# Sums of weight blocks: from accumulating DRAM transfers to VectorE additions, in a two-layer encoder on one core

## The chip, the cores and the metric

The kernel runs on one core of a Trainium2 chip. The metric is the device time of one execution in microseconds; the median of three executions is given. Engines by the names of the profile: PE (TensorE, matrix products), PEld (its weight loads), DVE (VectorE), ACT (ScalarE), POOL (GpSimd), SP (SyncE, which issues most transfers). Sixteen DMA engines move data between DRAM (HBM) and the on-chip memory SBUF; transfers that SP issues are on queue q1, those that GpSimd issues on queue q0.

## The reference

A two-layer encoder in float32 over 16 + 256 = 272 tokens of width 2048. One layer, cut to what matters here:

```python
h = rmsnorm(x)
q, k, v, f, ga, gf = split(h @ w_in)
a_br = attention(q, k, v) @ w_attn_br
s_br = real(fft2(f)) @ w_four
x = x + (sigmoid(ga) * a_br + sigmoid(gf) * s_br) @ w_out
h2 = rmsnorm(x)
up = h2 @ w_up                       # (272, 2 * 5632)
u_gate = dwconv3(up[:, :5632])
u_val = up[:, 5632:]
x = x + (silu(u_gate) * u_val) @ w_down
```

The output is the 256 real tokens after the second layer, whose feed-forward therefore needs 256 tokens only.

## The kernel before

**Weights as chunks.** All weights are read once, in the order in which TensorE uses them, as chunks of 128x1024 float32, 512 KB each. `order` (L172) lists the groups of matmuls with their chunks. For each chunk, SP loads it into a buffer `raw` (L233 to L245, four buffers), ScalarE rounds it to `wh` (L280), VectorE computes the rest `wl` = raw - wh (L283, three buffers each), and TensorE multiplies three times, with `wh` and the activations' high part, `wh` and their low part, `wl` and their high part (L352 to L354): 24 matmuls to a chunk. `advance` and `pump` keep the splits two chunks ahead of TensorE (LOOK = 2) and the loads four buffers ahead of these. In layer 0 the Fourier weights are folded by two VectorE additions before their split (`fold_w`, L268).

**Stages.** In the time of the profile: layer 0's projections, attention and Fourier part, gates and output projection up to about 540 us; its feed-forward (264 chunks: `ps_ug`, `ps_uv`, `ps_d`) to about 1336 us; layer 1's mixing part to about 1830 us; its feed-forward to the end.

**Block products.** The second feed-forward computes part of its products, those of `w_dn` (most rows of `w_down`) and `w_vn` (part of `w_up`), by a seven-product scheme on 2x2 blocks of weights, in place of eight products (`PRODUCTS`, L52). Four of the seven need sums of weight blocks. With w(h, k) for block k of column half h:

- sum 0 = w(0,0) + w(1,0)
- sum 1 = sum 0 + w(1,1)
- sum 2 = w(1,1) + w(1,0)
- sum 3 = w(0,1) + sum 1

They are made in DRAM, `fv` (4 x 8 chunks) for `w_vn`, `ft` (4 x 20 chunks) for `w_dn`, and layer 1 loads them as ordinary chunks (112 of them).

**How the sums are made.** `weight_sums` (L533) is a generator. For each sum and pair of chunks it lets GpSimd issue a transfer from DRAM to DRAM that copies the first summand (1 MB), and then another that adds the second summand to it in DRAM (`accum_op`). Ahead of each issue stands a one-column copy `tick` on GpSimd that reads the last `wl` (L538), so that the transfer starts in step with the splits. 56 copies and 56 accumulations.

**Pace.** `step` (L294) is called after every six matmuls of a chunk of 24 (four steps to a chunk). It advances one background generator of the list `shadow` whose count has run out, and, separately, `weight_sums`, every `slow[2]` steps: 15 to 45, set by stage, from the first Fourier gate of layer 0 until the sums are done in layer 1's feed-forward.

**Folds.** `prefold` (L513) runs in the background of the first feed-forward. It loads 32 chunks of layer 1's Fourier weights (`pfi`) over SP's queue, folds each by four VectorE additions of 128x256 (L528) and stores it to `fw` over SP's queue, one in about 28 steps.

**Order.** Instructions of an engine run in the order of its queue. A scheduler places most of them; those under `keep_in_program_order` stay in the order of the program among themselves.

Of the kernel before, what the change touches and what calls it, by code (L numbers as in the profile page):

```python
# [10 lines left out]
F32 = mybir.dt.float32  # L11
F32R = mybir.dt.float32r
AF = mybir.ActivationFunctionType
ALU = mybir.AluOpType
AX = mybir.AxisListType

P = 128
# [5 lines left out]
KT = D // P  # L23
# [3 lines left out]
NG = 8  # L27
# [5 lines left out]
CW = 4  # L33
MG = 2
FF_SPLIT = (24, 20)
SETS = (12, 8)
NQ = sum(SETS)
# [19 lines left out]
NV = KT // 2  # L57
# [3 lines left out]
FIRSTS = [sum(SETS[:i]) for i in range(len(SETS))]  # L61
# [6 lines left out]
def _branch(text):  # L68
# [3 lines left out]
BRANCH_ORDER = (  # L72
    _branch("ga0 ga1 ga2 ga3 gf0 gf1 s0 gf2 a0 s1 gf3 a1 s2 ga4 a2 s3 gf4 a3"),
    _branch("s4 a4 ga5 gf5 s5 a5 ga6 gf6 s6 a6 ga7 gf7 s7 a7"),
)
# [83 lines left out]
def encoder_kernel(ctx, tc, xT, params, consts, bmat, cfold, csign, w_fl, w_f64c, w_in, w_abr, w_four, w_f64, w_out, w_up, w_down, w_vn, w_dn, w_dt, out):  # L159
    nc = tc.nc  # L160
# [5 lines left out]
    fw = dram.tile([2 * KT, P, CW, MG * P], F32, name="fw")  # L166
    ft = dram.tile([4, NQ, P, CW, MG * P], F32, name="ft")
    fv = dram.tile([4, NV, P, CW, MG * P], F32, name="fv")
# [4 lines left out]
    for l in range(DEPTH):  # L173
# [13 lines left out]
        for half in range(2):  # L187
            for kind, j in BRANCH_ORDER[half]:
                w, off, n = {"ga": (w_in, IN_GA, KT), "gf": (w_in, IN_GF, KT), "s": (w_four, 0, 8), "a": (w_abr, 0, 8)}[kind]
# [24 lines left out]
    chunks, folded, mix, summed = [], set(), {}, {}  # L214
    t, done = 0, 0
    for key, chs in order:
        for j, ch in enumerate(chs):
            n = 0
            if key[0] == 1 and key[1] in ("t", "ug", "uv"):
                n = due(t) - done  # L220
                t += 1
            if n:
                mix[key, j] = n
                for s, p, k in PRODUCTS[done:done + n]:
                    if p in (3, 4, 5, 6):
                        summed[len(chunks)] = (s > 0, (3, 0, 1, 2)[p - 3], k // 2)
                    chunks.append(pchunks[done])
                    done += 1
                first_mix = min(first_mix, len(chunks) - n) if done > n else len(chunks) - n
            if key[:2] == (0, "s"):  # L230
                folded.add(len(chunks))
            chunks.append(ch)
    st = {"raw": 0, "fetch": 0, "next": 0, "grp": 0}  # L233
# [13 lines left out]
    todo, ready_sums = [], set()  # L247
# [26 lines left out]
    def split_w(i, a, b, parts="hl"):  # L274
        if i not in splits:
            splits[i] = tuple(wp.tile([P, CW, MG * P], F32R, tag=t, name=f"{t}{i}") for t in ("wh", "wl"))
        h, lo = splits[i]
        r = raws[i]
        if "h" in parts:
            nc.scalar.copy(h[:, a:b], r[:, a:b])  # L280
        st["wl"] = lo
        if "l" in parts:
            nc.vector.tensor_tensor(lo[:, a:b], r[:, a:b], h[:, a:b].bitcast(F32), op=ALU.subtract)  # L283
            if b == CW:
                del raws[i]
# [3 lines left out]
    def push(gen, wait=0):  # L289
        shadow.append([wait, gen])  # L290

    slow = [0, None, 0]

    def step(force=False):  # L294
        if not force and slow[1] and slow[2]:
            slow[0] -= 1
            if slow[0] <= 0:
                slow[0] = slow[2]
                if next(slow[1], None) is None:
                    slow[1] = None  # L300
        for s in shadow:
            s[0] -= 1
        for s in list(shadow):
            if force or s[0] <= 0:
                try:
                    s[0] = next(s[1])
                except StopIteration:
                    shadow.remove(s)
                return
# [5 lines left out]
    def drain():  # L315
        while shadow:
            step(True)
# [136 lines left out]
    small = ctx.enter_context(tc.tile_pool(name="small", bufs=4))  # L454
# [55 lines left out]
        norm_split(m, goff)  # L510
        norm_sum(m)

    def prefold(pool):  # L513
        src = [w_fl[k] for k in range(KT)] + [w_four[1, j, c] for j in range(NG) for c in range(2)]
        outs = {}
        for j in range(len(src) + 1):
            if j < len(src):
                a = pool.tile([P, CW, MG * P], F32, tag="pfi", name=f"pfi{j}", bufs=2)
                nc.sync.dma_start(a, src[j])
            if j:  # L520
                nc.sync.dma_start(fw[j - 1], outs.pop(j - 1))
            yield 15
            if j < len(src):
                o = pool.tile([P, CW, MG * P], F32, tag="pfo", name=f"pfo{j}", bufs=2)
                for q, op in ((0, ALU.add), (1, ALU.subtract)):
                    for c in range(2):
                        half = (lambda t_, e: t_[:, 2 * c:2 * c + 2, e * P:(e + 1) * P]) if j < KT else (lambda t_, e: t_[:, 2 * e + c])
                        tc.keep_in_program_order(nc.vector.tensor_tensor(half(o, q), half(a, 0), half(a, 1), op=op))  # L528
                        yield 3
                outs[j] = o  # L530
            yield 1

    def weight_sums():  # L533
        rows = lambda ap: ap.rearrange("k p c m -> (k p) (c m)")

        def issue(out_, s, **kw):
            tick = small.tile([P, 1], F32, tag="tick", name="tick", bufs=1)
            tc.keep_in_program_order(nc.gpsimd.tensor_copy(tick, st["wl"][:, 0, 0:1].bitcast(F32)))  # L538
            tc.keep_in_program_order(nc.gpsimd.dma_start(out_, s, **kw))

        for f, wd, nq, q0, n in [(fv, w_vn, NV, 0, NV)] + [(ft, w_dn, NQ, q0, n) for q0, n in zip(FIRSTS, SETS)]:
            dst = lambda q, j: rows(f[q, 2 * j:2 * j + 2])
            w = lambda h, k, j: rows(wd[h, nq * k + 2 * j:nq * k + 2 * j + 2])
            kinds = ((0, lambda j: w(0, 0, j), lambda j: w(1, 0, j)),
                     (1, lambda j: dst(0, j), lambda j: w(1, 1, j)),
                     (2, lambda j: w(1, 1, j), lambda j: w(1, 0, j)),
                     (3, lambda j: w(0, 1, j), lambda j: dst(1, j)))
            for q, base, more in kinds:
                j0, j1 = q0 // 2, (q0 + n) // 2
                for j in range(j0, j1 + 1):  # L550
                    if j < j1:
                        issue(dst(q, j), base(j))
                        yield 1
                    if j > j0:
                        issue(dst(q, j - 1), more(j - 1), accum_op=ALU.add, max_dma_last_dim=4096)
                        ready_sums.add((f is ft, q, j - 1))
                        yield 1

    def norm_stats(holder, gap=0):
        am = small.tile([P, P // NM, NM], F32, tag="am", name="am", bufs=1)  # L560
# [23 lines left out]
        holder["tok2"] = tok2  # L584

    xr = lambda lo: (lambda kt: (xH[:, kt, lo:T], xL[:, kt, lo:T]))
    slow[1] = weight_sums()

    for l in range(DEPTH):
        last = l == DEPTH - 1  # L590
        lo = 14 if last else 0
# [4 lines left out]
        with tc.tile_pool(name=f"mix{l}", bufs=1) as mp:  # L596
# [567 lines left out]

            tha, thf, w64s = {}, {}, []
            for half in range(2):
                slow[2] = 0
                mH = mL = None
                for n_, (kind, i) in enumerate(BRANCH_ORDER[half]):
                    if half or n_ >= (8 if last else 4):  # L1170
                        slow[2] = 26 if last else 15
                    j = i - 4 * half
                    if kind == "ga":
                        tha[i] = gate("ga", i)
# [16 lines left out]
                    else:  # L1191
# [7 lines left out]
                        for m in range(MG):  # L1199
                            k = 2 * j + m  # L1200
                            t_, h_ = tha[i][:, m, lo:T], mH[:, k, lo:T]
# [1 line left out]
                            nc.vector.tensor_tensor(t_, t_, thf[i][:, m, lo:T], op=ALU.add)  # L1203
                            nc.scalar.copy(h_, t_)
                            nc.vector.tensor_tensor(mL[:, k, lo:T], t_, h_.bitcast(F32), op=ALU.subtract)  # L1205
                slow[2] = 22 if last else 20 if half else 15
                for mg in range(8):
                    ps = group((l, "o", half, mg), lambda kt: (mH[:, kt, lo:T], mL[:, kt, lo:T]), W)
                    for m in range(MG):
# [6 lines left out]
        with tc.tile_pool(name=f"ffn{l}", bufs=1) as fp:  # L1216
            hold = {}
            push(norm_stats(hold), 8)
            if not last:
                push(prefold(fp), 8)  # L1220
            def conv_gate(i):
                ps = group((l, "ug", i), xr(lo), W)
                until(hold, "tok2")
# [23 lines left out]
            for c, n in enumerate(() if last else FF_SPLIT):  # L1247
                gHL = fp.tile([P, FF_SPLIT[0], 2, T], F32R, tag="gHL", name="gHL")
                gH, gL = gHL[:, :, 0, :], gHL[:, :, 1, :]
                for i in range(k0 // MG, (k0 + n) // MG):  # L1250
                    cs = conv_gate(i)
                    ps = group((l, "uv", i), xr(0), T)
                    for m in range(MG):
                        j = 2 * i + m - k0
# [7 lines left out]
                        if c == len(FF_SPLIT) - 1:  # L1262
                            norm_in(mt, P_NM + (l + 1) * KT)
                k0 += n
            if not last:
                slow[2] = 0

            if last:
                X0, X1 = 26, 32
                XF = XT.rearrange("p k t -> p (k t)")  # L1270
# [16 lines left out]
                left = {(h, b): (1 if h == 1 and b < 2 else 2) * len(SETS) + 1 for h in range(2) for b in range(4)}  # L1287
# [84 lines left out]
                def products():  # L1372
                    late = []
                    until(hold, "tokens")
                    slow[2] = 45
                    make_ahead()
                    bank.extend([psum.tile([P, 512], F32, tag="aux", name=f"ps_p{i}{h}") for h in range(2)] for i in range(2))
                    for s_, p, q in PRODUCTS:
                        ps = bank[(p in (4, 2, 1)) ^ s_ % 2]
                        fresh = p in (0, 4, 1)  # L1380
                        wh, wl = (w.rearrange("p c m -> p (c m)") for w in next_split())
                        direct = s_ == 0 and p in plain
                        if direct:
                            k, h = plain[p]
                            a, b = xH[:, k + q, xt[h]], xL[:, k + q, xt[h]]
                        else:
                            a, b = made.pop((s_, p, q))
# [12 lines left out]
                        if (s_, q) in END:  # L1400
                            while late:
                                hand_out(*late.pop(0))
                            t_, c, minus = {0: (0, 0, 0), 4: (1, 2, 0), 5: (0, 2, 1), 2: (0, 2, 0), 6: (1, 2, 1), 1: (0, 0, 0), 3: (1, 0, 0)}[p]
# [4 lines left out]
                        yield  # L1408
                    assert not late

                slow[2] = 18
                st["products"] = products()
                st["pool"] = fp
                for i in UP_ORDER:
# [14 lines left out]
                    for m in range(0 if i in VPAIRS else MG):  # L1429
                        j = 2 * i + m  # L1430
                        cv = cs[m][:, lo2:T]
                        v = fp.tile([P, W2], F32, tag="v", name="v", bufs=2)
# [16 lines left out]
                for b in TAIL_ORDER:  # L1449
                    k, chs = order[st["grp"]]  # L1450
# [95 lines left out]
```

## Time and profile before

| | us |
|---|---|
| median of 3 runs | 2542.17 (2540.26 to 2542.8) |
| span of the profiled execution | 2544.3 |
| PE busy in it | 2528.2 (99%) |
| DVE busy | 1825.0 (72%) |
| ACT busy | 1319.8 (52%) |
| POOL busy | 132.3 (5%) |

The profiled execution's own time is its span; around it lies nothing that the profile shows, and the runs without a profile are about 2 us shorter. Matmuls overlap in the pipeline, so the busy time of PE is the time in which at least one was under way, and it says nothing of how fast each one ran; the windows give the number of matmuls beside it. DMA share is the mean over 16 engines of the time that packets took; packets on one engine can overlap, so that a short window can show more than 1.

A row of windows reads: stretch, its length, then busy time and (xcount) of PE, PEld, DVE, ACT and POOL, then granted TensorE clock, DMA share, and GB/s moved. A row of waits reads: who waited, at which tile and line, for whom: total us, times, longest us. A row of DMA queues reads: packets, MB, share. A row of issues reads: destination and source, queue, count, KB each, median us from issue to landing.

### The profile page before, as it was taken

The numbers are of one execution on the slowest core, as the hardware profiler recorded it, in microseconds if no ns is written. First come the engines' busy times: TensorE is split into PE (matmuls) and PEld (weight loads), VectorE is DVE, ScalarE is ACT, GpSimd is POOL, SyncE is SP. The second block draws the span as 40 slices with busy tenths as digits, with TensorE's granted clock in tenths as the row PEclk, the third lists the DMA queues.
The fourth block names the chain that finished last, engine by engine and source line by source line (L and its number), as shares of the span: only waits on it lengthen the run. The fifth ranks groups of instructions, "written<-read, shape, count | busy, mean of one in ns | idle before, by whom it ended". The sixth has DMA issues, their size and how long they took to land.

```text
span 2544.3 us, 47646 instructions
## 1 busy us (share of the span) xinstructions
PE 2528.2 (99%) x18992; PEld 2447.4 (96%) x18992; DVE 1825.0 (72%) x2889; ACT 1319.8 (52%) x1893; POOL 132.3 (5%) x265
## 2 busy tenths in 40 slices
PE   9999999999999999999999999999999999999999
PEld 8999999999999999999999999999988999888987
DVE  7687766776666556666558877666778778777788
ACT  5455434554444334444445555444676566656565
POOL 0000100000000000000000000000000000000000
PEclk9999999999999999999999999999999999999999
DMA  6546889989989998999875646887889888887787
GB/s 238 163 156 217 261 270 288 280 262 302 308 271 305 300 306 274 281 318 294 252 247 183 201 150 209 246 266 240 260 293 282 298 274 285 288 286 264 240 268 261
DMA packets 171215, 660.69 MB, mean 260 GB/s; under 512 B 19424, under 2 KB 24672, under 8 KB 170096
## 3 DMA queue, kind: packets, MB, share of 16 engines
q1 hardware_dynamic: 152528, 538.07, 61.3%
q0 software_dynamic: 17024, 117.45, 18.7%
q8 instruction: 149, 2.44, 0.4%
q10 hardware_dynamic: 1440, 2.13, 0.2%
q14 instruction: 74, 0.61, 0.1%
HBM read 635.91 MB, written 136.31 MB: 304 GB/s over the span
## 4 chain that ended last, share of the span: by engine, by line
PE 86%; DMA 2%; DVE 1%; ACT 1%; issue 0%; ACTq 0%; DVEq 0%
PE ps_p L1390 10%; PE ps_ug L353 7%; PE ps_ug L354 7%; PE ps_ug L352 7%; PE ps_uv L348 4%; PE ps_d L353 3%; PE ps_uv L353 3%; PE ps_d L352 3%; PE ps_uv L354 3%; PE ps_d L354 3%; PE ps_uv L352 3%; PE ps_o L353 2%; PE ps_o L354 2%; PE ps_o L352 2%; PE ps_uv L349 2%; PE ps_gf L354 2%
## 5 line engine op out<-in xcount | busy, mean ns | idle before, releaser
L283 DVE TENSOR_TENSOR wl<-raw,wh 128x1024 fp32r<-128x1024 f32 (+1 forms) x937 | 1129.7, 1217 | 567.5 <-ACT wh L280 559.5
L280 ACT CAST wh<-raw 128x1024 fp32r<-128x1024 f32 (+1 forms) x937 | 976.0, 1046 | 890.8 <-PE ps_ug L353 201.2
L353 PE MATMUL ps_ug<-xHL,wh 128*128 128x272 f32 (+1 forms) x1408 | 401.9, 285 | 0.0
L354 PE MATMUL ps_ug<-xHL,wl 128*128 128x272 f32 (+1 forms) x1408 | 401.4, 285 | 0.4 <-DVE wl L283 0.4
L352 PE MATMUL ps_ug<-xHL,wh 128*128 128x272 f32 (+1 forms) x1408 | 400.8, 285 | 0.0
L353 PEld LDWEIGHTS ps_ug<-xHL,wh 128*128 128x128 f32 x1408 | 264.7, 188 | 3.2
L352 PEld LDWEIGHTS ps_ug<-xHL,wh 128*128 128x128 f32 x1408 | 264.6, 188 | 3.2
L354 PEld LDWEIGHTS ps_ug<-xHL,wl 128*128 128x128 f32 x1408 | 264.7, 188 | 0.6 <-DVE wl L283 0.6
L353 PE MATMUL ps_uv<-xHL,wh 128*128 128x272 f32 x704 | 203.3, 289 | 0.0
L353 PE MATMUL ps_d<-gHL,wh 128*128 128x272 f32 x704 | 202.9, 288 | 0.0
L352 PE MATMUL ps_d<-gHL,wh 128*128 128x272 f32 x704 | 202.9, 288 | 0.0
L354 PE MATMUL ps_uv<-xHL,wl 128*128 128x272 f32 x704 | 202.6, 288 | 0.0
L352 PE MATMUL ps_uv<-xHL,wh 128*128 128x272 f32 x704 | 202.3, 287 | 0.0
L354 PE MATMUL ps_d<-gHL,wl 128*128 128x272 f32 x704 | 202.1, 287 | 0.0
L1390 PE MATMUL ps_p<-wh,opnd 128*128 128x512 f32 x688 | 187.8, 394 | 0.0
L348 PE MATMUL ps_uv<-xHL,wh 128*128 128x512 f32 x448 | 159.8, 395 | 0.0
L353 PE MATMUL ps_o<-mL,wh 128*128 128x272 f32 (+1 forms) x512 | 146.6, 286 | 1.3 <-DVE mL L1205 1.3
L352 PE MATMUL ps_ga<-xHL,wh 128*128 128x272 f32 (+1 forms) x512 | 147.8, 289 | 0.0
L352 PE MATMUL ps_gf<-xHL,wh 128*128 128x272 f32 (+1 forms) x512 | 146.9, 287 | 0.1
L354 PE MATMUL ps_gf<-xHL,wl 128*128 128x272 f32 (+1 forms) x512 | 146.0, 285 | 0.4 <-DVE wl L283 0.4
L353 PE MATMUL ps_ga<-xHL,wh 128*128 128x272 f32 (+1 forms) x512 | 146.1, 285 | 0.0
L353 PE MATMUL ps_gf<-xHL,wh 128*128 128x272 f32 (+1 forms) x512 | 146.1, 285 | 0.0
(372 smaller groups left out, 5871.4 us busy)
## 6 DMA issues: line engine op xcount, KB each, us to landing
raw<-in_w_up SPq DMA_DIRECT2D x320, 512.0 KB, 5.2
raw<-in_w_in SPq DMA_DIRECT2D x191, 512.0 KB, 4.2
raw<-in_w_down SPq DMA_DIRECT2D x88, 512.0 KB, 5.4
raw<-ft SPq DMA_DIRECT2D x80, 512.0 KB, 4.8
raw<-in_w_out SPq DMA_DIRECT2D x64, 512.0 KB, 5.6
ft<-in_w_dn POOLq DMA_DIRECT2D x30, 1024.0 KB, 12.0
raw<-in_w_dn SPq DMA_DIRECT2D x60, 512.0 KB, 4.7
raw<-in_w_abr SPq DMA_DIRECT2D x32, 512.0 KB, 4.8
```

What stands on the lines that cost most here:

```text
L280: nc.scalar.copy(h[:, a:b], r[:, a:b])
L283: nc.vector.tensor_tensor(lo[:, a:b], r[:, a:b], h[:, a:b].bitcast(F32), op=ALU.subtract)
L348: nc.tensor.matmul(o2, h[:, c, sl], ab, start=kt == 0, stop=False)
L349: nc.tensor.matmul(o, lo[:, c, sl], ab[:, 0, :], start=False, stop=kt == nk - 1)
L352: nc.tensor.matmul(o, h[:, c, sl], a, start=kt == 0, stop=False)
L353: nc.tensor.matmul(o, h[:, c, sl], b, start=False, stop=False)
L354: nc.tensor.matmul(o, lo[:, c, sl], a, start=False, stop=kt == nk - 1)
L1390: nc.tensor.matmul(ps[h], x, w[:, 512 * h:512 * h + 512], start=fresh and (s_, q) in BEGIN and first, stop=(s_, q) in END and end, skip_gr ...
```

## The change

`weight_sums`, `prefold`, the tick copies, `slow` and its settings go. In their place stands one generator `prepare`, which is pushed to the background list at the start of the first feed-forward. It first does the 32 folds, then the 112 sums, one chunk of 512 KB at a time. GpSimd issues all its transfers, loads and stores between DRAM and seven SBUF buffers `ws`. A fold is the same four additions as before. A sum is made in place on VectorE, in two additions of 128x512, from chunks that are in SBUF: each of the four blocks of a position is loaded once, and sums 1 and 3 take the sum made before them from its buffer. A fold's load is issued two jobs ahead, a sum's load four jobs ahead, and a job takes seven steps, every fourth one six. So all folds and sums now lie in the first feed-forward, and none elsewhere.

```diff
-        st["wl"] = lo
...
-    slow = [0, None, 0]
-
     def step(force=False):
-        if not force and slow[1] and slow[2]:
-            slow[0] -= 1
-            if slow[0] <= 0:
-                slow[0] = slow[2]
-                if next(slow[1], None) is None:
-                    slow[1] = None
...
-    def prefold(pool):
...
-    def weight_sums():
...
+    def prepare(pool):
+        tt = lambda *v, **kw: tc.keep_in_program_order(nc.vector.tensor_tensor(*v, **kw))
+        dma = lambda *v: tc.keep_in_program_order(nc.gpsimd.dma_start(*v))
+        tile_ = lambda n: pool.tile([P, CW, MG * P], F32, tag="ws", name=n, bufs=7)
+        folds = [(w_fl[k], k) for k in range(KT)] + [(w_four[1, j, c], KT + 2 * j + c) for j in range(NG) for c in range(2)]
+        sums = []
+        for f, wd, nq in ((fv, w_vn, NV), (ft, w_dn, NQ)):
+            for k in range(nq):
+                sums += [(wd[h, nq * e + k], (f, q, k)) for h, e, q in ((0, 0, 0), (1, 0, 2), (1, 1, 1), (0, 1, 3))]
+
+        def fold(held, n, j):
+            a, o = held[n], tile_(f"wo{n}")
+            for q, op in ((0, ALU.add), (1, ALU.subtract)):
+                for c in range(2):
...
+                    tt(half(o, q), half(a, 0), half(a, 1), op=op)
+                    yield 1
+            dma(fw[j], o)
+
+        def sum_up(held, n, f, q, k):
+            x, y = held[n], held[n + (1, -2, 1, -1)[q]]
+            for c in (0, 2):
+                tt(x[:, c:c + 2], x[:, c:c + 2], y[:, c:c + 2], op=ALU.add)
+                yield 1
+            dma(f[q, k], x)
+            ready_sums.add((f is ft, q, k))
+
+        for jobs, ahead, work in ((folds, 2, lambda h, n, to: fold(h, n, to)), (sums, 4, lambda h, n, to: sum_up(h, n, *to))):
+            held = {}
+            for n in range(len(jobs) + ahead):
+                if n < len(jobs):
+                    held[n] = tile_(f"wi{n}")
+                    dma(held[n], jobs[n][0])
+                left = 7 - n % 4 // 3
+                if n >= ahead:
+                    for v in work(held, n - ahead, jobs[n - ahead][1]):
+                        left -= v
+                        yield v
+                yield left
...
-    slow[1] = weight_sums()
...
-                push(prefold(fp), 8)
+                push(prepare(fp), 8)
```

More of the change, by code (lines that the diff above doesn't have):

```diff
@@ L225, in encoder_kernel @@
                     if p in (3, 4, 5, 6):
-                        summed[len(chunks)] = (s > 0, (3, 0, 1, 2)[p - 3], k // 2)
+                        summed[len(chunks)] = (s > 0, (3, 0, 1, 2)[p - 3], k)
                     chunks.append(pchunks[done])
@@ L511, in norm_in @@
         norm_sum(m)
-    def prefold(pool):
[L514 to L531, printed above, removed]
@@ L533, in weight_sums @@
-    def weight_sums():
[L534 to L557, printed above, removed]
@@ new lines, in prepare @@
+    def prepare(pool):
[11 more added lines that the diff above has]
+                for c in range(2):
+                    half = (lambda t_, e: t_[:, 2 * c:2 * c + 2, e * P:(e + 1) * P]) if j < KT else (lambda t_, e: t_[:, 2 * e + c])
+                    tt(half(o, q), half(a, 0), half(a, 1), op=op)
[20 more added lines that the diff above has]
+                yield left
@@ L1166, in encoder_kernel @@
             for half in range(2):
-                slow[2] = 0
                 mH = mL = None
-                for n_, (kind, i) in enumerate(BRANCH_ORDER[half]):
-                    if half or n_ >= (8 if last else 4):
-                        slow[2] = 26 if last else 15
+                for kind, i in BRANCH_ORDER[half]:
                     j = i - 4 * half
@@ L1205, in encoder_kernel @@
                             nc.vector.tensor_tensor(mL[:, k, lo:T], t_, h_.bitcast(F32), op=ALU.subtract)
-                slow[2] = 22 if last else 20 if half else 15
                 for mg in range(8):
@@ L1264, in encoder_kernel @@
                 k0 += n
-            if not last:
-                slow[2] = 0
             if last:
@@ L1374, in products @@
                     until(hold, "tokens")
-                    slow[2] = 45
                     make_ahead()
@@ L1409, in products @@
                     assert not late
-                slow[2] = 18
                 st["products"] = products()
```

## The prediction

> **What bounds the kernel now.** I read the page first, then the waits of TensorE, then the stages by windows, then the DMA queues of single stages. The page:
>
> ```profile
> span 2544.3 us, 47646 instructions
> PE 2528.2 (99%) x18992; PEld 2447.4 (96%) x18992; DVE 1825.0 (72%) x2889; ACT 1319.8 (52%) x1893; POOL 132.3 (5%) x265
> ...
> q1 hardware_dynamic: 152528, 538.07, 61.3%
> q0 software_dynamic: 17024, 117.45, 18.7%
> ```
>
> TensorE is idle for 2544.3 - 2528.2 = 16.1 us. No edit changes its list of matmuls, so 16.1 us, plus what the clock lost, is all there is to win, while any starving is a loss. Queue q0 holds only the weight sums. Its 117.45 MB take 18.7% of the engines' span, so 18.7 / 117.45 = 0.159% per MB; q1 pays 61.3 / 538.07 = 0.114%. The waits of TensorE, whole span:
>
> ```profile
> PE ps_f L420 <- ACT wh L280: 4.7, 2, 4.4
> PE ps_a L354 <- DVE wl L283: 2.8, 2, 2.6
> PE ps_s L388 <- DVE wl L283: 1.4, 2, 0.8
> PE ps_o L353 <- DVE mL L1205: 1.3, 1, 1.3
> PE ps_fa L652 <- DVE E L631: 1.1, 1, 1.1
> PE ps_ug L354 <- DVE wl L283: 0.4, 1, 0.4
> PE ps_gf L354 <- DVE wl L283: 0.4, 1, 0.4
> PE ps_uv L349 <- DVE wl L283: 0.3, 1, 0.3
> ```
>
> `ps_f` (start of the program), `ps_o` and `ps_fa` wait for something other than a weight split; the change touches none of them. The five waits for `wl` come to 2.8 + 1.4 + 0.4 + 0.4 + 0.3 = 5.3 us. Where they sit, in windows of 10 us in the mixing part of layer 0:
>
> ```profile
> 240.00:250.00 10.00, 10.00 (x82) 10.00 (x81) 6.19 (x12) 3.50 (x5) 0.69 (x2) 1.00 1.01 360
> 260.00:270.00 10.00, 9.96 (x81) 9.82 (x80) 8.00 (x17) 5.14 (x10) 0.69 (x2) 1.00 1.10 351
> 270.00:280.00 10.00, 7.41 (x52) 7.19 (x52) 4.48 (x7) 2.76 (x4) 0.00 (x0) 0.90 0.49 159
> 280.00:290.00 10.00, 10.00 (x78) 10.00 (x78) 9.11 (x17) 6.04 (x12) 1.45 (x2) 0.93 0.85 225
> 300.00:310.00 10.00, 9.00 (x70) 8.57 (x69) 7.90 (x13) 4.30 (x6) 0.70 (x2) 1.00 0.99 369
> ```
>
> The columns are the length, PE, PEld, DVE, ACT and POOL busy, granted clock, DMA share, GB/s. DMA is full (1.01 to 1.10) just before TensorE falls to 7.41 of 10 us, and after that gap the clock is 0.90 and 0.93, another 10 x (0.10 + 0.07) = 1.7 us. In the stretch from 203 to 330 us the waits and the queues say why:
>
> ```profile
> DVE wpm L271 <- DMA raw<-in_w_four: 13.8, 3, 6.2
> ```
>
> ```profile
> q0 software_dynamic: 1385, 10.92, 31.5%
> ...
> raw<-in_w_four SPq DMA_DIRECT2D x8, 512.0 KB, 7.2
> ```
>
> VectorE waits up to 6.2 us for Fourier weights that land 7.2 us after issue, while the weight sums hold 31.5% of the DMA engines. Everywhere else TensorE is full. The first feed-forward, about 540 to 1336 us, is where all sums will go (same columns; the last row is the end of the kernel with almost no q0):
>
> ```profile
> 540.00:829.00 289.00, 289.00 (x2307) 288.92 (x2307) 192.46 (x301) 132.31 (x172) 18.59 (x39) 1.00 0.90 295
> 829.00:1000.00 171.00, 171.00 (x1365) 171.00 (x1364) 91.98 (x121) 63.01 (x65) 10.89 (x24) 1.00 0.92 296
> 1000.00:1215.00 215.00, 215.00 (x1719) 215.00 (x1718) 143.18 (x220) 95.62 (x123) 13.09 (x28) 1.00 0.91 294
> 1215.00:1336.00 121.00, 121.00 (x966) 121.00 (x965) 67.61 (x90) 53.74 (x72) 7.28 (x18) 1.00 0.80 248
> ...
> 2220.00:2500.00 280.00, 280.00 (x1660) 248.03 (x1658) 221.19 (x277) 173.99 (x218) 0.71 (x1) 1.00 0.81 266
> ```
>
> TensorE has not one idle microsecond there; a matmul takes 289 / 2307 = 0.125 us, a chunk of 24 matmuls 3.01 us, a background step (six matmuls) 0.75 us. DMA is at 0.90, so this is also the stage with least room.
>
> **Removed outside the first feed-forward.** All 56 copies, 56 accumulations and 112 tick copies on GpSimd go, from 203 us to 2220 us. GpSimd is at 5%, so ticks cost nothing now. What the path wins is the waits for `wl`, 5.3 us, and the clock's 1.7 us: 7.0 us. Bounds: 0, if the Fourier chunks are late by their own burst, and 16.1 + 1.7 - 4.7 - 1.3 - 1.1 = 10.7 us, if everything but the three foreign waits went. I take 6: the stalls stand right behind full DMA windows, and without a third of the load the chunks should land as they do in quieter stretches, but each still needs two fold additions on VectorE.
>
> **Moved and added: transfers.** In the first feed-forward the weights are 264 chunks of 512 KB (0.524 MB), 138 MB; the folds 32 loads and 32 stores, 34 MB, now on GpSimd's queue instead of SP's; the sums 112 loads and 112 stores, 117 MB. Together 289 MB in 796 us, 364 GB/s, against (289x295 + 171x296 + 215x294 + 121x248) / 1000 = 229 MB now. The price of a MB is what matters:
>
> ```profile
> q1 hardware_dynamic: 17851, 65.00, 62.8%
> q0 software_dynamic: 2771, 19.92, 27.2%
> ...
> raw<-in_w_up SPq DMA_DIRECT2D x91, 512.0 KB, 6.2
> pfi<-in_w_fl SPq DMA_DIRECT2D x15, 512.0 KB, 6.7
> ft<-in_w_dn POOLq DMA_DIRECT2D x7, 1024.0 KB, 12.1
> fw<-pfo SPq DMA_DIRECT2D x13, 512.0 KB, 5.4
> ```
>
> These are 540 to 829 us. Plain traffic: 0.628 x 289 us for 65.0 MB, 358 GB/s at share 1. Sums as they are now: 0.272 x 289 for 19.92 MB, 253 GB/s. A store (5.4 us to landing) is no dearer than a load (6.7). At the plain price 289 MB need 807 us of 796, a share of 1.01. That alone does not stop TensorE, because the share adds up packets that overlap, and goes above 1:
>
> ```profile
> 720.00:728.00 8.00, 8.00 (x66) 8.00 (x65) 7.09 (x12) 4.26 (x7) 0.76 (x2) 1.00 1.18 455
> 932.00:956.00 24.00, 24.00 (x193) 24.00 (x192) 12.20 (x15) 8.42 (x8) 1.78 (x4) 1.00 1.03 363
> 1392.00:1416.00 24.00, 23.95 (x207) 23.38 (x206) 23.32 (x33) 16.90 (x26) 0.12 (x1) 1.00 0.83 258
> ```
>
> From 932 to 956 us 363 GB/s pass, the rate needed on average, at full TensorE, with dear accumulations among them; 455 GB/s pass for 8 us. From below the cost is 0. From above, the last stage's 266 / 0.81 = 328 GB/s as a ceiling gives 289 / 0.328 = 881 us, 85 us more. I take 0: the 24 us row is nearest in rate and mix.
>
> The Trainium skill (DMA: Bandwidth & Descriptors, Specifications) gives a core about 358 GB/s of HBM bandwidth; by it the stage would take 289 / 0.358 = 807 us, 11 us longer. The rows of 363 and 455 GB/s speak against that as a hard limit over 24 and 8 us; no run here shows 364 GB/s over 796 us.
>
> **Added: VectorE.** 112 sums in two halves are 224 additions of 128x512. The nearest rows (the first fence for the whole program, the second for 545 to 1336 us):
>
> ```profile
> L280 ACT CAST wh<-raw 128x1024 fp32r<-128x1024 f32 (+1 forms) x937 | 976.0, 1046 | 890.8 <-PE ps_ug L353 201.2
> ...
> L271 DVE TENSOR_TENSOR wpm<-raw 128x512 f32<-128x512 f32 x32 | 21.1, 688 | 20.9 <-DMA raw<-in_w_four 20.7
> ```
>
> ```profile
> L283 DVE TENSOR_TENSOR wl<-raw,wh 128x1024 fp32r<-128x1024 f32 x263 | 322.2, 1225 | 276.2 <-ACT wh L280 274.9 <-issue 0.7
> L528 DVE TENSOR_TENSOR pfo<-pfi 128x256 f32<-128x256 f32 x128 | 51.6, 419 | 0.0
> ```
>
> 224 x 0.688 = 154 us onto 495 us of VectorE (the four windows), 649 of 796, 82%. Tightest is the start, where the 32 folds, spread over 680 us now, come one in 6.75 steps, 5.1 us: 4 x 0.419 = 1.68 us in 5.1 (33%) where before it was about 8%, so 192 / 289 = 67% becomes some 92%. From 1392 to 1416 us VectorE ran at 97% and TensorE lost 0.05 us. The splits run two chunks ahead of TensorE, 6 us, less a cast of about 1.05 us and a split of 1.2 us: nearly 4 us of backlog before a matmul waits. I take 0 for it, 10 us as the bad end (6% of the 170 us that the folds last).
>
> **Added: waits.** On VectorE an addition now waits for its load, and behind it in order stands the next `wl` split, for which TensorE waits. A sum's second operand is asked for three jobs ahead, 15 us, a fold's operand at least 14 steps, 10.5 us, against 6.7 us landing for such a load now. On GpSimd a load waits for the store that frees its buffer, at the closest two jobs earlier, 10 us against 5.4; behind it stand only transfers of this kind. GpSimd issues 288 transfers; a present issue is
>
> ```profile
> L539 POOL DMA_DIRECT2D ft<-in_w_dn x60: 502/728/955, 589.3 to 2156.1; - x60
> ```
>
> 288 x 0.73 = 210 us of 760: covered. SP is rid of 64 transfers and keeps the order of the rest. The last sum stands beside chunk 425 of the chunks 168 to 431, about 20 us before the stage ends, so nothing of layer 1 waits.
>
> **The sum.** 2544.3 - 6 = 2538 for the profiled execution. The median of the runs is 2542.2, 2.1 below the span, so I forecast 2536 us.
>
> **Rivals.**
> 1. *DMA becomes the bound of the first feed-forward* (slower). Place: 540 to 1336 us; it decides once the engines carry less than the 364 GB/s needed. For it: the highest average of any long row is 296 GB/s, at 0.92 already; against it: the 363 GB/s row. At 358 GB/s the stage is 11 us longer, 2536 + 11 = 2547; at 328 it is 85 us longer, 2621. Chance 0.27, mostly at the lower end.
> 2. *VectorE's backlog* during the folds. For it the 92%, against it the row at 97%. Up to 10 us: 2536 + 4 to 2536 + 10, about 2541. Chance 0.14.
> 3. *The stalls are not the sums' doing*: a chunk of a Fourier group feeds 16 matmuls, half of them of half the length, where others feed 24, so these groups call for chunks faster and may stall anyway. Then nothing is won, 2542. For it: VectorE also folds there; against it: DMA at 1.01 to 1.10 just before. Chance 0.09.
>
> The forecast itself has 0.5. A difference under 0.2%, 5 us, can't be told from none. Faster: 0.5. Within: rivals 2 and 3 and a little of 1, 0.24. Slower: 0.26. The likeliest case's own range is 2532 to 2539 (gains of 3 to 10 us). The range of 8 in 10 runs from 2532, below which hardly anything is left, to 2560, which leaves out the dear part of rival 1.
>
> **What would show it.** Right: no waits for `wl` between 240 and 310 us and no clock below 1.00 there; TensorE equal to the length of the windows from 540 to 1336 us, at DMA near 1.0 and VectorE near 82%; landings of `raw` there no longer than about 8 us. Wrong: TensorE below the length in that stage with a wait for `wl`; if those splits wait for DMA `raw`, it is rival 1; if VectorE is without gaps, or an addition waits for its load, it is rival 2 or the new waits.

## The result, and the profile after

| | median, us | runs |
|---|---|---|
| before | 2542.80 (2540.26 to 2547.36) | 21 |
| changed | 2538.43 (2536.28 to 2540.98) | 21 |

The ratio is 0.9982, with a 95% interval from 0.9976 to 0.9989: 4.4 us faster, within the range of the prediction (2532 to 2560) and 2.4 us above its point. That is 0.18%, which the prediction's own bound of 0.2% calls no difference, but the interval excludes 1. An unedited second measurement on another chip gave 2538.50 against 2542.38, ratio 0.9982 (0.9973 to 0.9991).

This is the page after. TensorE's idle time is 2535.6 - 2526.2 = 9.4 us, 16.1 before. Queue q0 now carries 151 MB at 15.8% of the span, where 117 MB cost 18.7%: 0.105% per MB in place of 0.159%.

```profile
span 2535.6 us, 47924 instructions
...
PE 2526.2 (100%) x18992; PEld 2445.7 (96%) x18992; DVE 1952.5 (77%) x3113; ACT 1317.9 (52%) x1893; POOL 174.5 (7%) x329
...
q1 hardware_dynamic: 143312, 504.51, 57.5%
q0 software_dynamic: 41472, 151.01, 15.8%
```

The waits of TensorE over the whole span. Of 5.3 us of waits for `wl`, 0.3 are left, and the wait of 1.3 us for `mL`, which the prediction had called foreign, is gone too:

```profile
PE ps_f L411 <- ACT wh L280: 4.6, 2, 4.5
PE ps_fa L636 <- DVE E L615: 0.7, 1, 0.7
PE ps_uv L340 <- DVE wl L282: 0.3, 1, 0.3
```

The windows that showed the stalls in layer 0's mixing part. TensorE is full, the clock whole, and the DMA share 0.5 to 0.7:

```profile
240.00:250.00 10.00, 10.00 (x83) 10.00 (x82) 7.42 (x13) 3.39 (x4) 0.00 (x0) 1.00 0.71 225
...
260.00:270.00 10.00, 10.00 (x83) 10.00 (x82) 8.29 (x15) 4.72 (x8) 0.00 (x0) 1.00 0.62 211
270.00:280.00 10.00, 10.00 (x84) 10.00 (x82) 7.74 (x13) 4.93 (x8) 0.00 (x0) 1.00 0.63 209
280.00:290.00 10.00, 10.00 (x83) 10.00 (x82) 7.97 (x17) 5.23 (x10) 0.00 (x0) 1.00 0.55 188
...
300.00:310.00 10.00, 10.00 (x84) 10.00 (x83) 9.80 (x21) 5.85 (x11) 0.00 (x0) 1.00 0.51 166
```

From 203 to 330 us VectorE's waits for Fourier chunks have fallen from 13.8 us, the longest 6.2, to 5.5 and 2.3:

```profile
DVE wpm L271 <- DMA raw<-in_w_four: 5.5, 3, 2.3
```

And the first feed-forward, which has taken all of the work: up to 384 GB/s at a share of about 1, and still TensorE is busy for the whole of each window:

```profile
540.00:829.00 289.00, 289.00 (x2307) 288.92 (x2307) 236.24 (x411) 131.58 (x170) 57.87 (x108) 1.00 0.97 362
829.00:1000.00 171.00, 171.00 (x1363) 171.00 (x1363) 119.87 (x154) 62.34 (x63) 36.30 (x68) 1.00 1.01 384
1000.00:1215.00 215.00, 215.00 (x1718) 215.00 (x1718) 177.35 (x264) 95.88 (x125) 44.29 (x83) 1.00 1.00 381
1215.00:1336.00 121.00, 121.00 (x964) 121.00 (x964) 87.97 (x128) 54.16 (x73) 17.72 (x35) 1.00 0.84 317
```

Since all these kernels run the same 18992 matmuls in the same order, the start of the same matmul can be compared between two traces, counted from the first one of each. Lead over the profiled execution of before, in us, at the matmul that it started at the given time (negative is earlier):

| kernel | 203 | 330 | 540 | 1336 | 1720 | 2050 | 2500 |
|---|---|---|---|---|---|---|---|
| changed | -0.7 | -8.0 | -9.4 | -8.9 | -8.6 | -10.7 | -9.3 |
| changed, again | -0.4 | -7.7 | -9.1 | -7.9 | -8.0 | -10.0 | -8.6 |

Of some 9 us, 7.3 come between 203 and 330 us, where the sums' transfers set in, and 1.4 between 330 and 540. The feed-forward gives back 0.5 to 1.2, and from 2050 us on 1.4 are lost slowly, with no wait to show for it. One execution of before is compared here, a long one (below), so its 9 us are more than the 4.4 of the medians.

### The profile page after: what moved, and what is told of

It is laid out like the page before. It is cut to its first block, busy times and chain, and to the rows that moved or that the text cites. A ratio compares the mean times of both kernels' runs of the same rounds, so it can differ in the third digit from the quotient of the medians.

```text
span 2535.6 us, 47924 instructions
## 1 busy us (share of the span) xinstructions
PE 2526.2 (100%) x18992; PEld 2445.7 (96%) x18992; DVE 1952.5 (77%) x3113; ACT 1317.9 (52%) x1893; POOL 174.5 (7%) x329
## 3 DMA queue, kind: packets, MB, share of 16 engines
q0 software_dynamic: 41472, 151.01, 15.8%
## 4 chain that ended last, share of the span: by engine, by line
PE 99%; DMA 1%; DVE 0%; ACT 0%; SPq 0%; issue 0%; POOL 0%; ACTq 0%
PE ps_p L1366 11%; PE ps_ug L344 7%; PE ps_ug L345 7%; PE ps_ug L343 7%; PE ps_uv L339 4%; PE ps_d L343 4%; PE ps_uv L344 3%; PE ps_d L344 3%; PE ps_d L345 3%; PE ps_uv L345 3%; PE ps_uv L343 3%; PE ps_gf L344 2%; PE ps_ga L344 2%; PE ps_gf L345 2%; PE ps_o L344 2%; PE ps_o L345 2%
## 5 line engine op out<-in xcount | busy, mean ns | idle before, releaser
L505 DVE TENSOR_TENSOR wi<-wi,wi 128x512 f32<-128x512 f32 x224 | 146.9, 685 | 0.0
```

What stands on the lines that cost most here:

```text
L505: tt = lambda *v, **kw: tc.keep_in_program_order(nc.vector.tensor_tensor(*v, **kw))
```

## The experiments

Medians stand beside that of the kernel before on the same chip, with the ratio to it.

**1. The accumulating kernel, its sums kept out of layer 0's mixing part.**

```diff
-                    if half or n_ >= (8 if last else 4):
-                        slow[2] = 26 if last else 15
+                    if last and (half or n_ >= 8):
+                        slow[2] = 26
...
-                slow[2] = 22 if last else 20 if half else 15
+                slow[2] = 22 if last else 0
...
                 push(prefold(fp), 8)
+                slow[2] = 13
```

> The kernel before, with its accumulating transfers held back until the first feed-forward, where one now goes out every 13 steps; layer 1 keeps the rest. Theory A (the gain is the stall that the sums' transfers cause in layer 0's mixing part): TensorE is busy for the whole of 144 to 330 us and the median is 2538 to 2540, though all transfers still accumulate. Rival B (the gain comes from layer 1, or from the transfers being plain): about 2542, as before. Rival D (the first feed-forward can't bear more accumulations): TensorE idle between 540 and 1336 us, 2545 or more.

2568.18 against 2542.87, ratio 1.0090 (1.0076 to 1.0105). Theory A's first half holds: TensorE is busy for 186.00 of 186 us from 144 to 330, the lead is -7.8 us at 540. Then rival D comes true: its windows show the first feed-forward starved, though it moves less than the changed kernel's does.

```profile
540.00:829.00 289.00, 281.79 (x2215) 279.46 (x2215) 183.56 (x290) 126.40 (x164) 27.86 (x57) 0.99 0.95 312
829.00:1000.00 171.00, 170.73 (x1361) 170.51 (x1360) 91.00 (x117) 61.54 (x63) 16.64 (x36) 1.00 1.00 334
1000.00:1215.00 215.00, 208.51 (x1619) 206.90 (x1618) 132.57 (x208) 90.53 (x118) 20.85 (x42) 0.98 0.96 311
```

At a DMA share of 0.95 to 1.00, transfers that accumulate pass 311 to 334 GB/s in total, the plain ones 362 to 384. So loads and stores through SBUF, in place of transfers that copy and accumulate in DRAM, are what lets this stage hold all of the sums; they aren't what wins the time in layer 0.

**2 and 3. The changed kernel with the old transfers put back into layer 0's mixing part**, as 29 transfers from DRAM to a DRAM buffer `fd` that nobody reads, with their tick copies: once copies and accumulations, once copies alone. The tick copies come back with them, so these two runs don't tell ticks from transfers; a tick takes 0.18 us of GpSimd, and in run 9 ticks are back in layer 1 and cost nothing that shows.

```diff
+                    issue(dst(q, j - 1), more(j - 1), accum_op=ALU.add, max_dma_last_dim=4096)
...
+                    if not last and (half or n_ >= 4):
+                        slow[2] = 15
```

> The changed kernel, with 29 transfers of 1 MB (copies and accumulations as before, into a DRAM buffer that nobody reads) put back into layer 0's mixing part at the old pace. Theory A: TensorE idle 2 to 5 us again between 240 and 310 us, DMA share near 1 just before, median 2541 to 2544. Rival B: 2538.5, as the changed kernel.

> As the run before, but the second transfer of each pair copies and doesn't add: the same count, and the same MB moved. If the double price of an accumulated MB makes the stall (theory A1), most of it is gone: 2538.5 to 2540, DMA share between 240 and 310 us well under 1. If any 1 MB transfer in the way does it (A2): 2541 to 2544, as with accumulation.

Accumulating: 2541.65, ratio to before 0.9997 (0.9988 to 1.0005). Copies alone: 2540.47, ratio 0.9993 (0.9984 to 1.0002). In both, VectorE's waits for Fourier chunks are back, 11.6 and 10.5 us from 203 to 330 us. The windows of the first, with the clock's fall behind the stall, and those of the second, where the stalls are shorter, the first of them comes later, and the DMA share is 0.86 before it:

```profile
260.00:270.00 10.00, 9.96 (x80) 9.82 (x80) 7.86 (x17) 5.01 (x9) 0.69 (x2) 1.00 1.11 344
270.00:280.00 10.00, 8.16 (x53) 7.95 (x52) 5.37 (x7) 2.93 (x4) 0.00 (x0) 0.83 0.58 195
```

```profile
270.00:280.00 10.00, 9.72 (x77) 9.51 (x77) 7.13 (x10) 3.70 (x5) 1.06 (x2) 1.00 0.86 309
280.00:290.00 10.00, 9.13 (x73) 8.78 (x72) 9.59 (x21) 6.01 (x12) 0.67 (x2) 1.00 0.45 170
```

Both kernels have a tick tile, so by run 11 below they are to be held against 2536.36, not 2538.43. Accumulation then costs 2541.65 - 2536.36 = 5.3 us, copying 4.1; the leads below give 5.2 and 3.8. Neither A1 nor A2 alone: 1 MB transfers in this place cost about 4 us even as plain copies. The double price of an accumulated MB (in the trace of before, a packet of 4 KB that accumulates takes 327 ns, a plain one 159) adds about 1 us, which the runs barely separate from none.

**4 and 5. How near the ceiling the stage runs:** a job every 6, and every 5 steps.

```diff
-                left = 7 - n % 4 // 3
+                left = 6
```

> The changed kernel with a job every 6 steps (4.5 us) in place of 6.75: 1.05 MB in 4.5 us are 232 GB/s, with the weights' 174 GB/s 406 GB/s while jobs last. If the DMA ceiling is the 415 GB/s that the changed kernel's best windows show: no loss, 2538 to 2541, share about 1. If it is nearer its average of 382: the sums fall behind, VectorE waits for their loads and TensorE for VectorE, 2545 to 2560.

> A job every 5 steps (3.8 us): 279 + 174 = 453 GB/s wanted, above every 24 us window seen. If 415 GB/s is a ceiling, the 151 MB of jobs need 151/0.241 = 626 us where the steps give 550: up to 76 us of waits on VectorE, and behind them on TensorE, 2560 to 2615. If waits are hidden by the splits' lead, or the ceiling is no ceiling: 2538 to 2542.

2558.16 against 2544.04, ratio 1.0051 (1.0034 to 1.0068), 18 to 20 us over the changed kernel (18 by the ratios, 20 by the medians, which are of different chips), and 2616.65, ratio 1.0288 (1.0265 to 1.0311), just beyond what was expected. The waits at pace 6, 540 to 1330 us:

```profile
POOL wi L506 <- DMA ft<-wi: 255.1, 54, 10.2
...
ACT wh L280 <- DMA raw<-in_w_up: 104.5, 54, 4.9
DVE wl L282 <- ACT wh L280: 81.7, 77, 2.8
...
DVE wi L505 <- DMA wi<-in_w_dn: 51.5, 17, 5.7
...
DVE wo L505 <- DMA wi<-in_w_four: 10.7, 6, 2.9
...
PE ps_uv L345 <- DVE wl L282: 9.7, 11, 1.9
```

VectorE stands before an addition whose load has not landed, the splits stand behind it, and TensorE behind them. These loads go out late, because GpSimd waits for the stores that free their buffers: 255.1 us, against 37.6 in the changed kernel. The weights' own loads take no longer, 7.7 us from issue to landing for `w_up` against 7.6, but ScalarE waits for them more than before (104.5 us against 20.8). That isn't what holds the splits: they wait less for a cast than in the changed kernel (81.7 us against 149.8). Windows of the two kernels in the middle of the stage, pace 6 first:

```profile
829.00:1000.00 171.00, 167.08 (x1319) 165.74 (x1318) 116.80 (x153) 59.24 (x59) 38.29 (x73) 1.00 1.01 388
1000.00:1215.00 215.00, 207.69 (x1639) 205.51 (x1638) 174.07 (x263) 90.76 (x118) 49.02 (x92) 1.00 1.00 389
```

```profile
829.00:1000.00 171.00, 153.53 (x1169) 150.38 (x1169) 112.95 (x153) 54.42 (x56) 41.23 (x78) 0.98 1.01 388
```

Whether 406 or 453 GB/s are wanted, 388 or 389 pass. Windows of 455 GB/s are bursts; 389 is what this mix sustains over 171 to 215 us. The seven buffers could be a limit too. The total speaks against it: it is the same at both paces, although at pace 5 TensorE takes its weights more slowly (153.53 us busy of 171 against 167.08), so that more of it is jobs. More buffers were not tried.

**6. The transfers of folds and sums on SP instead of GpSimd.**

```diff
-        dma = lambda *v: tc.keep_in_program_order(nc.gpsimd.dma_start(*v))
+        dma = lambda *v: tc.keep_in_program_order(nc.sync.dma_start(*v))
```

> The changed kernel with the 288 transfers of folds and sums issued by SP instead of GpSimd. If the queue matters (a store waits on VectorE's addition, a load on a store's landing, and behind them in order stand the weights' loads): raw chunks are issued late, TensorE waits in the first feed-forward, 2545 to 2600. If only the DMA engines count: 2538.

2577.57 against 2544.04, ratio 1.0132 (1.0117 to 1.0147): 38 to 39 us over the changed kernel, with not a byte more. SP's own waits between 540 and 1330 us:

```profile
SPq L506 <- DVE wo L505: 66.7, 24, 5.7
```

SP waits up to 5.7 us for a fold's addition (L506 issues the stores of folds and sums), and the weights' loads stand behind it: ScalarE waits 53.1 us for `raw` from `w_up`, 20.8 in the changed kernel. On GpSimd nothing that TensorE is in a hurry for stands there.

**7. Every addition of a sum done twice**, first as two of 128x256 into a scratch tile that nobody reads.

```diff
+                for i in (c, c + 1):
+                    tt(small.tile([P, T], F32, tag="sq", name="wx", bufs=2)[:, :MG * P], x[:, i], y[:, i], op=ALU.add)
                 tt(x[:, c:c + 2], x[:, c:c + 2], y[:, c:c + 2], op=ALU.add)
```

> The changed kernel with every addition of a sum done twice, the second time into a scratch tile that nobody reads: 448 additions of 128x256, about 0.33 us each where they stand one behind another, 150 us more onto 621 us of VectorE in the first feed-forward, 97% of 796. If VectorE has the slack that the forecast gave it (a backlog of 4 us is free): 2538 to 2548. If it was already near its bound: 2560 or more, VectorE without gaps and TensorE waiting for wl.

2572.02, ratio 1.0106 (1.0091 to 1.0121): the second case, 32 to 34 us over the changed kernel. Its window:

```profile
1000.00:1215.00 215.00, 204.19 (x1586) 199.78 (x1585) 210.50 (x397) 90.80 (x116) 41.60 (x78) 1.00 0.97 350
```

VectorE is busy for 98% and TensorE loses 11 us. But the run asks for more than the 97% that was reckoned over the whole stage: from 720 to 1300 us, where the sums stand, the changed kernel's VectorE is busy for 450 of 580 us, and the extra additions took 170 us in place of 150. That is 620 us of work for 580, 107%, and the 40 us too many are about what was lost. So the run shows that more than VectorE can do delays TensorE; it doesn't test the forecast's backlog of 4 us, nor a demand just under 100%. The changed kernel asks 177 of 215 us here, 82%.

**8. The changed kernel again**, as the measure for the next two on their chip.

> The changed kernel, unedited, on the chip of the two next runs, as their measure: 2538 to 2540, 4 to 5 us under the kernel before on that chip.

2538.50 against 2542.38.

**9. Accumulations put back into layer 1** (edit as in 2, at the old pace of 26, 22, 18 and 45 steps).

> The changed kernel with 32 copies and accumulations of 1 MB put back into layer 1 at the old pace (30 lay there before), none in layer 0. The mixing part of layer 0 gave back about 3 us of the 4.4 (2541.65). If the rest of the gain is layer 1's, this costs 1 to 2 us over the changed kernel on the same chip, with waits of TensorE for wl or mL between 1500 and 2220 us. If layer 1 never cared: the changed kernel's time within 0.5 us.

2536.27 (2535.44 to 2538.85), ratio 0.9974 (0.9964 to 0.9984). Neither expectation: with more to do, this kernel is 2.2 us faster than the changed one beside it. These transfers cost layer 1 nothing that shows, and something else in this edit wins. The lead table says where: it keeps its -9.5 us from 2050 to 2500, where the changed kernel falls from -10.0 to -8.6.

**10. Pace 6.5**, `left = 7 - n % 2`.

> A job every 6.5 steps (4.9 us) in place of 6.75 (0 loss) and 6 (20 us more): 214 + 174 = 388 GB/s wanted, just the most that any long stage moved in the runs at pace 6 and 5. If 388 GB/s is the ceiling: 0 to 5 us over the changed kernel. If the loss grows evenly between 6.75 and 6: about 6 us.

2537.93, ratio 0.9984 (0.9975 to 0.9993): no loss. It moves 389 and 388 GB/s from 829 to 1215 us, at the ceiling, and TensorE is full:

```profile
829.00:1000.00 171.00, 171.00 (x1363) 171.00 (x1362) 121.45 (x156) 62.53 (x63) 37.66 (x71) 1.00 1.01 389
1000.00:1215.00 215.00, 215.00 (x1718) 215.00 (x1717) 179.32 (x267) 96.31 (x126) 46.84 (x88) 1.00 1.01 388
```

So the loss does not grow evenly: nothing up to 388 GB/s wanted, 18 to 20 us at 406.

**11 and 12. The place of the tiles.** The kernels with the slow loss are those without the one-column tile `tick`; without it all later tiles of SBUF lie 32 bytes lower, which moves them to the other half of 64 bytes. In the built programs the operands `opnd` of the block products stand at byte 222112 of a partition before (a multiple of 64, plus 32) and at 222080 in the changed kernel (a multiple of 64). One unused tile puts them back to 222112, and in the kernel before it moves them on to 222144, again a multiple of 64; `wl` stays where it is:

```diff
+    pad = small.tile([P, 1], F32, tag="pad", name="pad", bufs=1)
...
     nc.gpsimd.memset(mhalf, -0.5)
+    nc.gpsimd.memset(pad, 0.0)
```

> The changed kernel with one unused tile of 32 bytes per partition where the tick tile lay, so that all later tiles of SBUF stand where they stood before. The changed kernel and its pace 6.5 version lose about 1.8 us slowly between 2050 us and the end and 0.5 us in the second half of the first feed-forward, matmul by matmul and without any wait, against the kernel before and against the runs that have the tick tile. If the place of the tiles does it: the slow loss is gone, 2536 to 2537, as the run with accumulations back in layer 1 (2536.27). If GpSimd's or the DMA's extra work does it: 2538.5.

> The counterpart: the kernel before with the same unused tile, so that its later tiles stand 32 bytes further on, in the other half of 64 bytes, as in the changed kernel. If the place of the tiles does it: 1 to 3 us slower than before, 2544 to 2546, lost slowly after 2050 us. If not: as before, 2542.5.

The changed kernel with the tile: 2536.36 (2535.90 to 2536.76), against 2542.72, ratio 0.9970 (0.9959 to 0.9982). The kernel before with it: 2543.91, ratio 1.0003 (0.9994 to 1.0012), just under the 2544 to 2546 expected, and the times do not separate it from none. The trace does, in part. The products with `wl` between 2130 and 2480 us (busy us, mean ns), in the order before, changed, changed with the tile, before with the tile:

```profile
L1390 PE MATMUL ps_p<-wl,opnd 128*128 128x512 f32 x196 | 60.6, 391 | 0.0
```

```profile
L1366 PE MATMUL ps_p<-wl,opnd 128*128 128x512 f32 x198 | 62.0, 394 | 0.0
```

```profile
L1368 PE MATMUL ps_p<-wl,opnd 128*128 128x512 f32 x198 | 61.2, 390 | 0.0
```

```profile
L1392 PE MATMUL ps_p<-wl,opnd 128*128 128x512 f32 x196 | 61.4, 394 | 0.0
```

391 and 390 ns with the operands at one place, 394 at the other, whichever kernel it is. From start to start over all 344 such matmuls it is 232.1 ns in the changed kernel and 228.2 with the tile, 1.3 us in all; those with `wh` give 0.8 more. In the kernel before it is 228.2 ns, and 232.9 with the tile. The whole lead, and that of the kernels that the table above lacks:

| kernel | 330 | 540 | 1336 | 2050 | 2500 |
|---|---|---|---|---|---|
| changed, with the tile | -6.7 | -7.9 | -7.9 | -10.1 | -10.1 |
| accumulations back in layer 1 | -6.6 | -7.8 | -7.8 | -9.5 | -9.5 |
| accumulations back in layer 0 | -1.9 | -2.7 | -2.7 | -4.9 | -5.0 |
| copies in layer 0 | -2.8 | -4.1 | -4.1 | -6.3 | -6.4 |
| before, with the tile | -1.5 | -3.1 | -3.5 | -3.8 | -1.0 |

The first four have the tiles where they were before, and none loses anything after 2050 us. The last has them moved and loses 2.8 us there, 0.8 of them in a wait for `wl`. The changed kernel with the tile beats the one without it and the kernel before; run 9's is as fast (2536.27).

## Why the prediction was right, point by point

- **The gain.** Taken as 6 us, from the stalls behind full DMA windows. With the tiles in their old place it is 2542.72 - 2536.36 = 6.4. Runs 1, 2 and 9 show its source: away in layer 0, all of the early lead; back in layer 0, 5.3 us lost; back in layer 1, nothing. So rival 3 falls: without the transfers the Fourier groups don't stall. The mechanism was right, and the size is that of the kernel whose tiles stay in place.
- **A wait that was called foreign.** About 1 us more seems to be won elsewhere (2541.65 in run 2 against before's 2542.87, which the interval doesn't separate from none). The leads place it at 1720 to 2050 us, where TensorE of the kernel before waits 1.3 us for `mL`. The prediction said that the change doesn't touch this wait. It stands in all three kernels that keep the old sums (before 1.3 us, run 12 0.9, run 1 2.4 with that for `mH`), and in none of the others, not in run 9's either, which has transfers there. What removes it is open.
- **What the forecast missed.** "The median of the runs is 2542.2, 2.1 below the span" mixes two executions, and the runs without a profile are not 2 us shorter than a span. In every later run whose span is known, the time lies above it, by 1.7 to 2.5 us (changed: 2537.81 for a span of 2535.6), and by 1.7 to 1.9 for the kernel before. So its profiled execution, 2544.3, was one of about 2546.1, near the slow end of its 21 runs. The profile's gain, 8.7 us, and the median's, 4.4, differ mostly by that. That the point lay only 2.4 us off is in part luck: the scale was 3.9 us too low, and the gain over that slow execution, with the tiles in their old place, was 2546.1 - 2536.4 = 9.7 us, 3.7 more than the 6 taken. The two errors all but cancel.
- **The 2 us of tile places** were in no term. The order of instructions was the same and was taken for the same speed. 2538.43 - 2536.36 = 2.1 us is about what is left of the point's error.
- **Transfers.** 364 GB/s on average, share 1.01 and no loss were forecast; (289x362 + 171x384 + 215x381 + 121x317) / 796 = 365 GB/s, a mean share of 0.97 and no loss came. The choice between 0 and 85 us was right, with little room: a job every 6 steps in place of 6.75 costs 18 to 20 us, one every 6.5 nothing.
- **By which way rival 1 decides** was mis-stated. It was to be late weights. Runs 4 and 5 show late summands: VectorE waits for them, ahead of the splits in its order. The Trainium skill's figure of about 358 GB/s to a core (DMA: Bandwidth & Descriptors, Specifications) is passed here by 381 to 384 GB/s over 386 us; the ceiling that these runs show is 389.
- **VectorE.** 154 us on 495 were forecast, 649. The windows show 236 + 120 + 177 + 88 = 621. The additions last 685 ns, as forecast, but in the trace neighbouring instructions of VectorE overlap by some 83 ns, so durations can't be added to busy time. In the folds 92% were forecast; from 550 to 710 us it was 134.15 of 160, 84%. That nothing was lost was right. What the rival's backlog would have cost is not shown: run 7 asks for more than VectorE can do.
- **The added waits.** A load was to land in 6.7 us as before; over GpSimd's queue at this load it takes 9.2 to 11.0. The 10.5 us that a fold has are less than the 11.0 of the loads from `w_four`:

```profile
DVE wo L505 <- DMA wi<-in_w_four: 9.1, 6, 2.3
```

  Six waits of up to 2.3 us on VectorE, all inside the lead of the splits. The step was right in the end, and the landing was mis-sized by 2.5 to 4.3 us.
- **GpSimd** issued 288 transfers at 537 ns, 155 us, where 210 were forecast, and held nothing up. Landings of `raw` from `w_up` took 7.6 us, under the 8 that were named. Run 6 bears out that the move off SP counts.

## What to carry to other kernels

When TensorE is full in one stage and stalls in another, background transfers belong where it is full, if the stage's whole demand, in GB/s by its own pace, stays under what a long window has sustained; here 388 GB/s were free and 406 cost 18 to 20 us. Additions and transfers that wait for each other go on queues where nothing urgent stands behind them. Before a profile is held against a median, ask whether its execution is a typical one, and after removing a tile, ask what moved in SBUF.

## What the runs showed of the hardware that was not expected

- The place of a matmul operand in SBUF changes its rate: 128x512 products whose operand moved by 32 bytes, onto a multiple of 64, went from 228.2 ns, start to start, to 232.1 and 232.9. Why was not tried.
- At a DMA share of about 1, the mix with transfers that copy and accumulate in DRAM passed 311 to 334 GB/s, loads and stores through SBUF 381 to 389. A packet of 4 KB that accumulates took 327 ns in the kernel before, a plain one 159.
- Behind a stall of TensorE the granted clock can fall, so that the stall costs more than its length: 0.90 and 0.93 in the windows of 10 us at the stall of 2.6 us before, 0.83 in run 2 at one of 1.8 us. It doesn't always: in run 7 the clock is 1.00 from 1000 to 1215 us, with stalls of up to 2.5 us.
